# Joined: the output projection's low parts on VectorE between the norm's steps, with late modulation tiles, and substitution on blocks of 32 over 100 partitions

## The chip, the core and the metric

The kernel runs on one core of a Trainium2 chip. A core has a matrix engine (TensorE, PE in the profile, with its weight loads as PEld), three engines for elementwise work (VectorE or DVE, ScalarE or ACT, GpSimd or POOL), a queue engine that starts most transfers (SyncE or SP) and 16 DMA engines. The metric is the device time of one execution in microseconds (us); the median of several executions counts.

## What is computed

One layer of a streaming encoder for two sequences: 1024 tokens of a new stream ("prompt") and 64 tokens that follow 256 cached ones ("sample"). Width 1024; a conditioning vector per sequence gives six modulation vectors. The reference, cut to what the change touches:

```python
mod = jax.nn.silu(c) @ w_ada + b_ada
sh1, sc1, gt1, sh2, sc2, gt2 = jnp.split(mod, 6, axis=-1)
h = _rms_norm(x, norm1_g) * (1 + sc1[:, None]) + sh1[:, None]
proj = h @ w_in
...
def step(s, inp):
    r_t, w_t, k_t, v_t, kk_t, a_t = inp
    sa = jnp.einsum('bhvk,bhk->bhv', s, -kk_t)
    s = (s * w_t[:, :, None, :]
         + sa[..., None] * (kk_t * a_t)[:, :, None, :]
         + v_t[..., None] * k_t[:, :, None, :])
    return s, jnp.einsum('bhvk,bhk->bhv', s, r_t)
...
mix = jnp.concatenate([y_rwkv, y_fox], axis=-1) @ w_out
x = x + gt1[:, None] * mix
h2 = _rms_norm(x, norm2_g) * (1 + sc2[:, None]) + sh2[:, None]
ffn = (jax.nn.silu(h2 @ w_ffn_gate) * (h2 @ w_ffn_up)) @ w_ffn_down
x = x + gt2[:, None] * ffn
```

The recurrence `step` (8 heads of 64) is computed in chunks of 64 tokens. Within a chunk it needs the inverse of a 64 x 64 unit triangular matrix, one for each chunk and head.

## The kernel before

The tokens are worked in two halves, half 0 with 512 columns (8 chunks) and half 1 with 576 (8 chunks of the prompt and the sample as a ninth). All large products are in fp32r with each operand split into a high and a low part, so that one product is three matmuls: high by high, high by low, low by high (`mm3`, L294 to L296 for the projections). A weight tile is loaded to `wraw`, its high part `whi` is cast by ScalarE (L212), its low part `wlo` is the difference (L216), on VectorE or, with `pool_lo` set, on GpSimd.

The stages in the trace of before, in order: start and norm (0 to 42 us); the projections of both halves with the recurrence's blocks between them (42 to about 690); attention of both halves with the out projection of half 0 (700 to 940); the transition (940 to 1050: out projection of half 1, norm and operand sums `h2_make` of both halves, first FFN products); the FFN's gate and up products (1050 to 1490, `ffn`, in a Strassen-like form with the seven products of `fast_half`); the down projection (1490 to 1760). The projections' 1872 matmuls are called `pmm` in the profile, those of the out projection `po`, those of the FFN `pfa`, `pfb`, `pfc`, `pfe`, those of the down projection `pd`.

The modulation is 48 tiles of 128 columns of w_ada. A tile is 16 small matmuls (`pada`, L190) into four row groups, a copy `mrow`, a transpose on PE (L198) and a sum on VectorE. Tiles 0 to 15 are made at the start, tiles 16 to 47 stand in a list, `background`, from which the projections take one now and then. Tiles 40 to 47 hold gt2, which only the down projection reads.

The recurrence has four blocks j of two heads in each half: `rwkv_a` prepares a block, `rwkv_b` finishes it. In `rwkv_a` the products of keys, `pA` (L464), are masked into `At` (L466); for every chunk, head and half of a chunk the two 16 x 16 diagonal blocks go through DRAM (`dm`) into a layout with one block per partition (`mb`, 64 or 72 partitions), where VectorE inverts all of them at once by forward substitution: 15 steps of a product `tb` (L488) and an addition to `wb` (L490). The inverses and their transposes (L491) go through DRAM again (`dw`, `du`) and are gathered as `gt` and `inv` in `rwkv_b`. There three groups of 32 x 32 matmuls (in `small`, L523: pg1, pw1, pu1, in the profile `pg`, `pw` and `pu` with the operand `g`) join two 16-blocks to a 32-block, with a masked copy `g1` on VectorE (L530) and an addition (L535) between them; pgt and pu12 join two 32-blocks to a 64-block, and the recurrence over the chunks follows (`pR`, `pSA`, `pS`).

The order on each engine is fixed when the program is built: a framework emits the code in program order, every engine runs its own instructions in the order in which it got them, and waits by semaphores; tiles come from pools with a fixed number of buffers, and a load into a buffer waits for the last reader of the previous tile there. Transfers start in the order of SyncE's queue. Code that is to lie beside other code is written as a generator (`h2_make`, `fast_prep`), of which hooks take one step after each product.

In the transition of before, `h2_make(half 0)` is issued whole ahead of the out projection of half 1, whose low parts are on GpSimd (L216). `x1_sq` sums the squares of each finished column tile, `x1_rs` turns them to the norm's factor. `ffn` begins with half 0 of the first gate pair, during which `h2_make(half 1)` is worked off by a hook.

## Time and profile before

| quantity | value |
|---|---|
| median of 3 runs | 1759.04 us (1754.95 to 1759.44) |
| the profiled execution's own time | 1761.91 us |
| its span in the trace | 1760.2 us |
| mean granted clock of PE | 0.974 |
| moved by DMA | 207.10 MB |

The profile is of one execution. "Busy" is the time in which at least one instruction of an engine runs; waits do not count. Rows of instruction groups give line, engine, operation, output and inputs with their shape, count, busy time in us, mean ns of one, and the idle time of the engine just before them with what ended it. Rows of waits read: who waited, for whom, us, times, longest. Rows of the timeline start with start and length in us. The granted clock is that of PE, 1.00 being full speed.

### The profile page before, as it was taken

Reading aid. Unit: us, or ns where it says so; the run is one execution under the profiler, and the core shown is the slowest. Engines: PE = TensorE matmul, PEld = TensorE weight load, DVE = VectorE, ACT = ScalarE, POOL = GpSimd, SP = SyncE. Lnnn points to the kernel's source line nnn. Section 1 sums busy time; section 2 is a strip of 40 time slices with the busy share of each in tenths; the row PEclk is TensorE's granted clock in tenths of the full one; section 3 lists DMA queues with packets and bytes.
Section 4 is the critical chain, followed back from the end, with each engine's and each line's share of the span. In section 5 each row is a group of like instructions: output and inputs, shape, how many; then the busy total and the mean of one; then the engine's idle time right before and its main releaser. Section 6 shows DMA issues by size and latency. Waiting matters only on the chain.

```text
span 1760.2 us, 33567 instructions
## 1 busy us (share of the span) xinstructions
PE 1673.6 (95%) x12893; PEld 1454.0 (83%) x12893; DVE 1105.8 (63%) x2518; ACT 728.0 (41%) x1532; POOL 267.6 (15%) x468
## 2 busy tenths in 40 slices
PE   5999999999999998889999779999999999999999
PEld 3676666688888886666888779999999999999998
DVE  6676676757786753777876685556666654444434
ACT  4435454543555344566776363233333222112110
POOL 2102121121222122100212300000000000222221
PEclk9999999999999997889999899999999999999999
DMA  8435356642233336376663302222222224533313
GB/s 314 151 87 157 116 165 195 184 122 71 76 75 92 107 84 167 96 203 166 158 188 128 106 34 83 74 74 74 74 74 78 79 89 134 182 99 93 99 36 120
DMA packets 136143, 207.10 MB, mean 118 GB/s; under 512 B 64687, under 2 KB 72911, under 8 KB 135983
## 3 DMA queue, kind: packets, MB, share of 16 engines
q1 hardware_dynamic: 135982, 204.95, 39.1%
q8 instruction: 102, 1.67, 0.4%
q14 instruction: 59, 0.48, 0.1%
HBM read 157.65 MB, written 47.25 MB: 116 GB/s over the span
## 4 chain that ended last, share of the span: by engine, by line
PE 81%; DVE 7%; ACT 6%; issue 3%; DMA 3%; POOL 1%; SPq 0%; ACTq 0%; DVEq 0%; POOLq 0%
PE pd L1244 15%; PE pfc L1143 7%; PE pfe L1143 7%; PE pfa L1143 7%; PE pmm L294 5%; PE pmm L296 5%; PE pmm L295 5%; PE pfb L1143 4%; PE pav L952 2%; PE pbs L375 2%; PE ppt L930 2%; PE pA L464 2%; PE pS L613 1%; PE po L295 1%; PE po L294 1%
## 5 line engine op out<-in xcount | busy, mean ns | idle before, releaser
L216 POOL TENSOR_TENSOR wlo<-wraw,whi 128x512 fp32r<-128x512 f32 (+2 forms) x64 | 107.1, 1675 | 777.5 <-ACT whi L212 772.2
L294 PE MATMUL pmm<-hhi,whi 128*128 128x288 f32 (+1 forms) x624 | 220.3, 353 | 1.0 <-ACT pb L317 0.7
L295 PE MATMUL pmm<-hlo,whi 128*128 128x288 f32 (+1 forms) x624 | 216.8, 347 | 1.4 <-DVE hlo L272 1.4
L296 PE MATMUL pmm<-hhi,wlo 128*128 128x288 f32 (+1 forms) x624 | 215.6, 345 | 0.0
L212 ACT CAST whi<-wraw 128x1024 fp32r<-128x1024 f32 (+2 forms) x116 | 99.2, 855 | 234.8 <-PE pd L1244 168.1
L1244 PE MATMUL pd<-ah,whi 128*128 128x512 f32 (+1 forms) x528 | 173.3, 329 | 2.2 <-ACT ah L212 2.2
L1244 PE MATMUL pd<-al,whi 128*128 128x512 f32 (+1 forms) x528 | 174.1, 330 | 0.5 <-DVE al L216 0.5
L1244 PE MATMUL pd<-ah,wlo 128*128 128x512 f32 (+1 forms) x528 | 173.7, 329 | 0.0
L1248 DVE SCALAR_TENSOR_TENSOR x1t<-pd,mod,x1t 128x512 f32<-128x512 f32 x192 | 90.6, 497 | 132.1 <-PE pd L1244 131.0
L294 PEld LDWEIGHTS pmm<-hhi,whi 128*128 128x128 f32 x624 | 119.2, 191 | 14.3 <-ACT pb L317 2.5
L295 PEld LDWEIGHTS pmm<-hlo,whi 128*128 128x128 f32 x624 | 119.4, 191 | 11.1 <-DVE hlo L272 2.1
L296 PEld LDWEIGHTS pmm<-hhi,wlo 128*128 128x128 f32 x624 | 119.4, 191 | 10.2 <-issue 1.2
L1143 PE MATMUL pfc<-hh,hS 128*128 128x256 f32 (+1 forms) x352 | 102.3, 291 | 8.0 <-ACT hh L1045 5.6
L1244 PEld LDWEIGHTS pd<-ah,whi 128*128 128x128 f32 x528 | 99.8, 189 | 10.5 <-ACT ah L212 2.7
L1244 PEld LDWEIGHTS pd<-al,whi 128*128 128x128 f32 x528 | 99.8, 189 | 8.5 <-DVE al L216 0.7
L1244 PEld LDWEIGHTS pd<-ah,wlo 128*128 128x128 f32 x528 | 99.9, 189 | 7.5
L604 POOL TENSOR_SCALAR sd<-sv,pc 64x64 f32<-64x64 f32 x136 | 72.1, 530 | 202.7 <-DVE sv L617 190.3
L1143 PE MATMUL pfc<-hl,hS 128*128 128x256 f32 (+1 forms) x352 | 102.4, 291 | 0.0
L1143 PE MATMUL pfc<-hh,lS 128*128 128x256 f32 (+1 forms) x352 | 102.2, 290 | 0.0
L1143 PE MATMUL pfa<-hh,whi 128*128 128x256 f32 (+1 forms) x352 | 102.0, 290 | 0.0
L1143 PE MATMUL pfa<-hl,whi 128*128 128x256 f32 (+1 forms) x352 | 101.8, 289 | 0.0
L1143 PE MATMUL pfa<-hh,wlo 128*128 128x256 f32 (+1 forms) x352 | 101.4, 288 | 0.0
(360 smaller groups left out, 4471.6 us busy)
## 6 DMA issues: line engine op xcount, KB each, us to landing
wraw<-in_w_in_dram SPq DMA_DIRECT2D x52, 512.0 KB
wada<-in_w_ada_dram SPq DMA_DIRECT2D x48, 512.0 KB
as<-actscr SPq DMA_DIRECT2D x22, 544.0 KB
wraw<-in_w_gate_dram SPq DMA_DIRECT2D x22, 512.0 KB
wraw<-in_w_up_dram SPq DMA_DIRECT2D x22, 512.0 KB
wraw<-in_w_down_dram SPq DMA_DIRECT2D x40, 256.0 KB
wraw<-in_w_out_dram SPq DMA_DIRECT2D x16, 512.0 KB
actscr<-sg SPq DMA_DIRECT2D x22, 288.0 KB
```

Source lines behind the costliest of these rows:

```text
L212: nc.scalar.copy(hi, src)
L216: eng.tensor_tensor(lo, src, hi.bitcast(F32), op=ALU.subtract)
L294: nc.tensor.matmul(ps[0:M, 0:n], whi[:, k, 0:M], xhi[:, k, off:off + n], start=(k == 0), stop=False)
L295: nc.tensor.matmul(ps[0:M, 0:n], whi[:, k, 0:M], xlo[:, k, off:off + n], start=False, stop=False)
L296: nc.tensor.matmul(ps[0:M, 0:n], wlo[:, k, 0:M], xhi[:, k, off:off + n], start=False, stop=(k == kt - 1))
L375: nc.tensor.matmul(ps[:, 0:n], w, x[:, off:off + n], start=True, stop=True)
L464: nc.tensor.matmul(pa[h][:, i], kb[hp, c + i], rk[hp, c + i], start=True, stop=True)
L604: nc.gpsimd.tensor_scalar(sd[hsl[h]], sv[hsl[h], c, h], pc[hsl[h], c], None, op0=ALU.mult)
L930: nc.tensor.transpose(pt[0:rows, b - b0, t * P:t * P + qn], p[0:qn, b * P:b * P + rows], self.ident[0:qn, 0:qn])
L1143: nc.tensor.matmul(ps, l[:, k], r[:, s, k], start=(first and k == 0 and y == 0), stop=(k == 3 and y == 2), skip_group_check=True)
L1244: nc.tensor.matmul(ps[:, 0:n], w[:, i], x[:, t:t + n], start=(i == 0 and y == 0), stop=(i == len(fs) - 1 and y == 2))
L1248: nc.vector.scalar_tensor_tensor(dst, ps[:, so - off:so - off + l], self.mod[:, 40 + o, b:b + 1], dst, op0=ALU.mult, op1=ALU.add)
```

## The change

There are three parts.

Substitution. It runs on 32 x 32 diagonal blocks. Each block's inverse is held as two halves of 16 columns, one on partitions 0 to 31 (35 in half 1), one from partition 64 on, so that all instructions span 100 partitions; rows and columns are stored with even ones ahead of odd ones, and the two halves take the even and the odd columns, so that a step works on a rectangle that is the same for both. There are 31 steps of a product and an addition. The first operand `rk` and the mask `amask` are written in the permuted order. The tile `mb` is allocated once and cleared on GpSimd. pg1, pw1 and pu1 with their masked copy, addition and copies are gone, as are the transfers that cleared `dw` and `du`.

Transition. After attention, all low parts of weights are made on VectorE (this holds for the down projection's weights too). `h2_make(half 0)` is taken step by step between the column tiles of the out projection of half 1, the first two weight tiles of which are loaded ahead of it. w_gate's first pair is loaded and prepared one column tile earlier, w_up's first pair after the first half of the first FFN step.

Modulation and activations. Tiles 40 to 47 leave the background list. Tiles 40 to 43 are made behind `x1_rs` of half 1, tiles 44 to 47 behind half 0 of the first FFN step (`gap`). The first two activation tiles of the down projection are loaded at the last FFN step but one (`early`).

```diff
-                                        fill=0.0, base=0, pattern=[[1, 64]], channel_multiplier=-1)
+                                        fill=0.0, base=0, pattern=[[32, 2], [1, 2], [2, 16]], channel_multiplier=-1)
...
+        self.mb = r.tile([100, 32, 32], F32, name="mb", tag="mb")
+        nc.gpsimd.memset(self.mb, 0.0)
...
-        nc.vector.tensor_tensor(rk[:, 0:nch, 0:64], ch(kk), pp[:, 0:nch, 0:64], op=ALU.mult)
+        for x in (0, 32):
+            eo = lambda t: t[:, 0:nch, x:x + 32].rearrange("p c (t e) -> p c t e", e=2)
+            nc.vector.tensor_tensor(rk[:, 0:nch, x:x + 32].rearrange("p c (e t) -> p c t e", e=2), eo(ch(kk)), eo(pp), op=ALU.mult)
...
-        nb = 2 * ng
-        dm = self.dpool.tile([2, ng, 2, 16, 16], F32, tag="dm", name="dm")
+        nb = 2 * nch * 2
+        dm = self.dpool.tile([ng, 2, 32, 32], F32, tag="dm", name="dm")
         for h in range(2):
             for x in range(2):
-                for i in range(2):
-                    o = 32 * x + 16 * i
-                    nc.sync.dma_start(dm[i, h * nch:(h + 1) * nch, x].rearrange("g s t -> s g t"),
-                                      At[64 * h + o:64 * h + o + 16, 0:nch, 0, h, o:o + 16])
-        mb = self.rpool.tile([72, 16, 16], F32, tag="mb", name="mb")
-        nc.sync.dma_start(mb[0:2 * nb], dm.rearrange("i g x s t -> (i g x) s t"))
-        wb = self.rpool.tile([72, 16, 16], F32, tag="wb", name="wb")
-        tb = self.rpool.tile([72, 64], F32, tag="tb", name="tb")
-        nc.gpsimd.memset(wb[0:2 * nb], 0.0)
-        nc.gpsimd.affine_select(out=wb[0:2 * nb], in_=wb[0:2 * nb], compare_op=ALU.not_equal, fill=1.0, base=0,
-                                pattern=[[-1, 16], [1, 16]], channel_multiplier=0)
-        for s in range(15):
-            m = 15 - s
-            t_ = tb[0:2 * nb, 0:m * (s + 1)].rearrange("p (a b) -> p a b", b=s + 1)
-            nc.vector.tensor_tensor(t_, mb[0:2 * nb, s, s + 1:16].unsqueeze(2).to_broadcast([2 * nb, m, s + 1]),
-                                    wb[0:2 * nb, s:s + 1, 0:s + 1].to_broadcast([2 * nb, m, s + 1]), op=ALU.mult)
-            nc.vector.tensor_tensor(wb[0:2 * nb, s + 1:16, 0:s + 1], wb[0:2 * nb, s + 1:16, 0:s + 1], t_, op=ALU.add)
-        nc.vector.tensor_copy(mb[0:2 * nb], wb[0:2 * nb].rearrange("p s t -> p t s"))
+                o = 32 * x
+                nc.sync.dma_start(dm[h * nch:(h + 1) * nch, x].rearrange("g s t -> s g t"),
+                                  At[64 * h + o:64 * h + o + 32, 0:nch, 0, h, o:o + 32])
+        mb = self.mb
+        nc.gpsimd.memset(mb[32:64], 0.0)
+        if nb == 32:
+            nc.gpsimd.memset(mb[96:100], 0.0)
+        for p in (0, 64):
+            nc.sync.dma_start(mb[p:p + nb], dm.rearrange("g x s t -> (g x) s t"))
+        wb = self.rpool.tile([100, 32, 16], F32, tag="wb", name="wb")
+        tb = self.rpool.tile([100, 144], F32, tag="tb", name="tb")
+        nc.gpsimd.memset(wb, 0.0)
+        for p, n in ((0, 64), (64, 36)):
+            o = slice(p // 4, p // 4 + 16)
+            nc.gpsimd.affine_select(out=wb[p:p + n, o], in_=wb[p:p + n, o], compare_op=ALU.not_equal, fill=1.0,
+                                    base=0, pattern=[[1, 16], [-1, 16]], channel_multiplier=0)
+        m4 = mb.rearrange("p s (e t) -> p s e t", e=2)
+        w4 = wb.rearrange("p (e t) c -> p e t c", e=2)
+        for s in range(31):
+            o, e = (s + 1) // 2, s // 2 + 1
+            m, sh = 16 - o, [100, 2, 16 - o, e]
+            t_ = tb[:, 0:2 * m * e].rearrange("p (x a b) -> p x a b", x=2, b=e)
+            nc.vector.tensor_tensor(t_, m4[:, s, :, o:16].unsqueeze(3).to_broadcast(sh),
+                                    w4[:, s % 2, s // 2, 0:e].unsqueeze(1).unsqueeze(1).to_broadcast(sh), op=ALU.mult)
+            nc.vector.tensor_tensor(w4[:, :, o:16, 0:e], w4[:, :, o:16, 0:e], t_, op=ALU.add)
+        wt = mb.rearrange("p s t -> p (s t)")[:, 0:512].rearrange("p (s t) -> p s t", s=16)
+        nc.vector.tensor_copy(wt.rearrange("p s (t e) -> p s t e", e=2), wb.rearrange("p (e t) c -> p c t e", e=2))
 
         dw, du = [t[j % 2] for t in (self.dw, self.du)]
-        for i in range(2):
-            r, o = slice(i * nb, (i + 1) * nb), slice(16 * i, 16 * i + 16)
-            for d, t in ((dw, wb), (du, mb)):
-                nc.sync.dma_start(d[0:ng].rearrange("g x s t -> (g x) s t")[:, o, o], t[r])
+        for i, p in enumerate((0, 64)):
+            o = slice(16 * i, 16 * i + 16)
+            for e in range(2):
+                nc.sync.dma_start(dw[0:ng].rearrange("g x (s e) t -> (g x) e s t", e=2)[:, e, :, o],
+                                  wb[p:p + nb, 16 * e:16 * e + 16])
+            nc.sync.dma_start(du[0:ng].rearrange("g x s t -> (g x) s t")[:, o], wt[p:p + nb])
...
-        g1 = self.rpool.tile([P, 9, 32], F32, tag="g1", name="g1")
-        pg = small("pg1", (0, 1), lambda h, c, r, o: (At[r, c, 0, h, o], gt[r, c]))
-        for h in range(2):
-            hs = slice(64 * h, 64 * h + 64)
-            nc.vector.tensor_tensor(g1[hs, 0:nch], pg[h][hs, 0:nch],
-                                    self.qmask[hs].unsqueeze(1).to_broadcast([64, nch, 32]), op=ALU.mult)
-        pg = small("pw1", (0,), lambda h, c, r, o: (inv[r, c, r], g1[r, c]))
-        for h in range(2):
-            r = slice(64 * h, 64 * h + 32)
-            nc.vector.tensor_tensor(gt[r, 0:nch, 0:16], gt[r, 0:nch, 0:16], pg[h][r, 0:nch, 0:16], op=ALU.add)
-        pg = small("pu1", (0, 1), lambda h, c, r, o: (g1[r, c], inv[r, c, r]))
-        for h in range(2):
-            for x in range(2):
-                r = 64 * h + 32 * x
-                nc.scalar.copy(inv[r:r + 16, 0:nch, r + 16:r + 32], pg[h][r:r + 16, 0:nch, 16:32])
...
+            if i and i + 2 < len(src):
                 raw.append(self.fast_raw(src[i + 2]))
+            if i == len(src) - 2:
+                early()
             old, nw = gen, {}
-            gen = self.fast_prep(raw[i + 1], nw) if i + 1 < len(src) else iter(())
+            gen = self.fast_prep(raw[i + 1], nw) if 0 < i < len(src) - 1 else iter(())
...
+                    gap()
+                    raw.append(self.fast_raw(src[2]))
+                    gen = self.fast_prep(raw[1], nw)
...
-            self.background = [lambda t=t: self.ada_fin(self.ada_mm(t)) for t in range(16, 48)]
+            self.background = [lambda t=t: self.ada_fin(self.ada_mm(t)) for t in range(16, 40)]
...
+            self.pool_lo = False
             acc = None
             for o in range(KT):
                 acc = self.x1_sq(halves[0], o, acc)
-            for _ in self.h2_make(halves[0], self.x1_rs(halves[0], acc)):
-                pass
+            w1 = [self.load_w(A["w_out"][o], [P, KT, P]) for o in range(2)]
+            h2 = self.h2_make(halves[0], self.x1_rs(halves[0], acc))
             pair = lambda x: [A[x][i] for i in range(2)]
-            acc, raw, w = None, [], {}
+            acc, raw, w, ada = None, [], {}, []
             for o in range(KT):
-                self.outproj(halves[1], o, ("ab", "ce")[o % 2])
+                self.outproj(halves[1], o, ("ab", "ce")[o % 2], w1[o] if o < 2 else None)
                 acc = self.x1_sq(halves[1], o, acc)
+                next(h2, None)
+                if o in (0, 2):
+                    next(h2, None)
+                if o == 4:
+                    raw.append(self.fast_raw(pair("w_gate")))
                 if o == 5:
-                    raw.append(self.fast_raw(pair("w_gate")))
-                if o == 6:
                     for _ in self.fast_prep(raw[0], w):
                         pass
-            raw.append(self.fast_raw(pair("w_up")))
+            for _ in h2:
+                pass
+            ada = [(t, self.ada_load(t)) for t in range(40, 44)]
             rs = self.x1_rs(halves[1], acc)
+            def ada_run(part):
+                old = None
+                for t, r in part:
+                    new = self.ada_mm(t, r, "b")
+                    if old:
+                        self.ada_fin(old)
+                    old = new
+                self.ada_fin(old)
+            def gap():
+                ada_run(ada[4:])
+                raw.append(self.fast_raw(pair("w_up")))
+            ada_run(ada)
+            ada += [(t, self.ada_load(t)) for t in range(44, 48)]
...
+            early_s = top.enter_context(ExitStack())
+            def early():
+                h2s[2].close()
+                self.spool.pools["as"] = L(early_s, "sas0", 2)
+                for f in range(2):
+                    pre.append(self.act_load(f, None))
```

How the instructions move is shown at three places, as rows of each engine's program order (line, operation, output and inputs, shape, count of equal rows).

TensorE at the end of the projections' stage, in the last block of half 1. `pg`, `pw` and `pu` with the operand `g` are the three groups of the 32-column combine, `pgt` the product that first uses the block's inverse, `pkv` and `pkvs` transposes of attention's values, `plora` a projection of the last output gates. Before:

```order
L523 MATMUL pg_8390<-gt,At 32x32 x15
L523 MATMUL pw_8431<-g_8389,inv_693 32x32 x9
L523 MATMUL pu_8453<-inv_693,g_8389 32x32 x18
L523 MATMUL pw_8430<-g_8389,inv_693 32x32 x2
L817 MATMUL pkv<-ident,fv 128x128 x4
L523 MATMUL pw_8430<-g_8389,inv_693 32x32 x7
L523 MATMUL pgt<-gt,At 32x32 x9
L523 MATMUL pu_8452<-inv_693,g_8389 32x32 x16
L823 MATMUL pkvs<-ident,fv 64x128
L523 MATMUL pu_8452<-inv_693,g_8389 32x32 x2
L549 MATMUL pu_8517<-inv_693,gt 32x32 x9
L523 MATMUL pgt<-gt,At 32x32 x9
```

After:

```order
L362 MATMUL plora<-z,wg 128x288
L810 MATMUL pkv<-ident,fv 128x128 x4
L362 MATMUL plora<-z,wg 128x288
L816 MATMUL pkvs<-ident,fv 64x128
L532 MATMUL pgt<-gt,At 32x32 x9
L542 MATMUL pu_7855<-inv_690,gt 32x32 x9
L532 MATMUL pgt<-gt,At 32x32 x9
L560 MATMUL pkbt<-ident,kb 128x128 x9
L542 MATMUL pu_7856<-inv_690,gt 32x32 x9
```

The three groups are gone; `pgt` now directly follows the gathered inverse.

VectorE in the transition, during the norm of half 0. `x_0` is half 0's tile, of which L1040 makes the norm and L1044 (after: L1037) the differences and low parts; L992 (after: L985) adds a finished out projection of half 1 to `x_1`. Before:

```order
L992 SCALAR_TENSOR_TENSOR x_1_11730<-po,mod,x_1_11730 128x224
L992 SCALAR_TENSOR_TENSOR x_1_11730<-po,mod,x_1_11730 128x64
L1040 SCALAR_TENSOR_TENSOR x_0_9704<-x_0_9704,g_162,nrs 128x512 x8
L992 SCALAR_TENSOR_TENSOR x_1_11730<-po,mod,x_1_11730 128x224
L992 SCALAR_TENSOR_TENSOR x_1_11730<-po,mod,x_1_11730 128x64
L1044 TENSOR_TENSOR hl_11726<-x_0_9704,hh_11725 128x1024
L992 SCALAR_TENSOR_TENSOR x_1_11730<-po,mod,x_1_11730 128x288
L1044 TENSOR_TENSOR x_0_9704<-x_0_9704 128x4x256
```

After:

```order
L1037 TENSOR_TENSOR x_0_9042<-x_0_9042 128x4x256
L216 TENSOR_TENSOR wlo<-wraw,whi 128x1024
L995 TENSOR_TENSOR nsq<-nsq 128x576
L1037 TENSOR_TENSOR hl_11070<-x_0_9042,hh_11069 128x1024 x2
L1037 TENSOR_TENSOR x_0_9042<-x_0_9042 128x4x256
L985 SCALAR_TENSOR_TENSOR x_1_11074<-po,mod,x_1_11074 128x288
L216 TENSOR_TENSOR wlo<-wraw,whi 128x1024
```

The low parts of w_out (`wlo`), which before stand on GpSimd, now stand on VectorE between the norm's steps.

TensorE in the first FFN step, half 0, at the passage from the product `pfe` to the product `pfb`. Before:

```order
L1143 MATMUL pfe<-hl_11726,hS_12268 128x256
L1143 MATMUL pfe<-hh_11725,lS_12269 128x256
L1143 MATMUL pfb<-hh_11725,hS_12264 128x256
L1143 MATMUL pfb<-hl_11726,hS_12264 128x256
L1143 MATMUL pfb<-hh_11725,lS_12265 128x256
```

After (L1136 is L1143 of before):

```order
L1136 MATMUL pfe<-hl_11070,hS_11547 128x256
L1136 MATMUL pfe<-hh_11069,lS_11548 128x256
L190 MATMUL pada<-wada,ct 32x128 x16
L198 MATMUL pada<-ident,mrow 128x128 x2
L190 MATMUL pada<-wada,ct 32x128 x16
L198 MATMUL pada<-ident,mrow 128x128 x2
L1136 MATMUL pfb<-hh_11069,hS_11543 128x256
L1136 MATMUL pfb<-hl_11070,hS_11543 128x256
```

Modulation tiles now stand between two of the step's products.

More of the change, by code (lines that the diff above doesn't have):

```diff
@@ L87, in consts @@
         nc.vector.reciprocal(sg, sg)
-        self.ct = self.cmid.tile([P, KT, 32], F32, name="ct")
+        self.ct = c.tile([P, KT, 32], F32, name="ct")
         nc.gpsimd.memset(self.ct, 0.0)
@@ L344, in rwkv_persist @@
         self.gt = r.tile([P, 9, 32], F32, name="gt", tag="gt")
-        self.qmask = self.fper.tile([P, 32], F32, name="qmask")
-        nc.vector.tensor_reduce(self.qmask[:, 0:1], self.ident.rearrange("p (q i s) -> p i q s", i=2, s=16)[:, 1],
-                                axis=AX.XY, op=ALU.add)
-        nc.vector.tensor_copy(self.qmask[:, 1:16], self.qmask[:, 0:1].to_broadcast([P, 15]))
-        nc.gpsimd.memset(self.qmask[:, 16:32], 0.0)
-        zero = self.inv[0].rearrange("p c t -> p (c t)")[0:72, 0:512]
-        for t in self.dw + self.du:
-            nc.sync.dma_start(t.rearrange("g x s t -> (g x s t)").rearrange("(p t) -> p t", p=72), zero)
+        self.mb = r.tile([100, 32, 32], F32, name="mb", tag="mb")
+        nc.gpsimd.memset(self.mb, 0.0)
         self.pp = r.tile([P, 9, 65], F32, name="pp", tag="pp")
@@ L975, in load_mix, with outproj @@
             self.split(mh[:, m, 0:n], ml[:, m, 0:n], t[:, 0:n], pool_lo=False)
-    def outproj(self, hf, o, tags=("mm",)):
-        wh, wl = self.load_w(self.A["w_out"][o], [P, KT, P])
+    def outproj(self, hf, o, tags=("mm",), w=None):
+        wh, wl = w or self.load_w(self.A["w_out"][o], [P, KT, P])
         for x, (off, n) in enumerate(hf.chunks):
@@ L1157, in fast_half, with ffn @@
                 h(x)
-    def ffn(self, halves, raw, w, h2gen, mid):
+    def ffn(self, halves, raw, w, h2gen, gap, early, mid):
         nc, A = self.nc, self.A
@@ L1197, in out, with prep @@
                                           sg[hf.i][:, 2 * q - 2:2 * q].rearrange("p q t -> p (q t)"))
-                hooks = [lambda x: next(gen, None) if self.STEPS[hf.i][x] else None]
+                def prep(x):
+                    for _ in range((0, 0, 0, 3, 2, 2, 1)[x] if i == 0 else self.STEPS[hf.i][x]):
+                        next(gen, None)
+                hooks = [prep]
                 if hf.i == 0:
@@ L1493, in x1_load @@
                     nc.sync.dma_start(x1a[o][:, hf.t0:hf.t0 + hf.n], self.x1scr[hf.i][:, o])
+            early_s = top.enter_context(ExitStack())
[4 more added lines that the diff above has]
+                    pre.append(self.act_load(f, None))
             def mid(x):
                 if x == 0:
-                    h2s[2].close()
                     h2s[0].close()
-                    self.spool.pools["as"] = R(ds, "sas", 2)
                     apools.append(MultiPool({t: R(ds, t + "0", 4) for t in ("ah", "al")}))
                     self.x1pools = [MultiPool({"x1": R(ds, "x1a", 4)})]
-                if x in (0, 1):
-                    pre.append(self.act_load(x, apools[0]))
-                if x in (3, 4):
-                    pre[x - 3] = self.act_split(pre[x - 3])
-                    pre.append(self.act_load(x - 1, apools[0]))
-                if x == 5:
+                    self.spool.pools["as"] = R(ds, "sas", 2)
+                    for f in range(2, 4):
+                        pre.append(self.act_load(f, None))
                     x1_load(0, self.x1pools[0])
-                if x == 6:
-                    pre[2] = self.act_split(pre[2])
-            self.ffn(halves, raw, w, self.h2_make(halves[1], rs), mid)
-            pre[3] = self.act_split(pre[3])
+                if 0 < x < 5:
+                    pre[x - 1] = self.act_split((pre[x - 1][0], apools[0]))
+            self.ffn(halves, raw, w, self.h2_make(halves[1], rs), gap, early, mid)
+            early_s.close()
             h2s[1].close()
```

5 lines of the change are left out of this document (2 added, 3 removed).

## The prediction

> **What bounds the kernel now.** First the page's busy shares and its slices, to see which engine has no room and where it does; then the chain of work that ended last.
>
> ```profile
> PE 1673.6 (95%) x12893; PEld 1454.0 (83%) x12893; DVE 1105.8 (63%) x2518; ACT 728.0 (41%) x1532; POOL 267.6 (15%) x468
> PE   5999999999999998889999779999999999999999
> DVE  6676676757786753777876685556666654444434
> PEclk9999999999999997889999899999999999999999
> PE 81%; DVE 7%; ACT 6%; issue 3%; DMA 3%; POOL 1%; SPq 0%; ACTq 0%; DVEq 0%; POOLq 0%
> ```
>
> TensorE (PE) is busy for 95% of the span, with dips only in slice 1, slices 16 to 18 and slices 23 and 24; 81% of the chain is PE. So whatever PE need no longer do counts in full, work that can be moved into the dips counts too, and work added to another engine counts only where PE has to wait for it. The change does all three: it takes matmuls out of the projections' stage, moves others into the dip near 1000 us, and loads VectorE (DVE). The next view is busy time by stretches over the projections' stage, 88 to 690 us (columns: stretch, length, busy time and instructions of PE, weight loads, DVE, ACT, POOL; granted clock, DMA share, GB/s).
>
> ```profile
> 88.00:264.00 176.00, 171.50 (x1411) 122.41 (x1411) 124.63 (x345) 81.08 (x169) 32.07 (x70) 0.98 0.46 131
> 264.00:396.00 132.00, 125.02 (x1162) 97.16 (x1160) 84.71 (x234) 66.92 (x158) 26.72 (x60) 0.95 0.58 167
> 396.00:572.00 176.00, 173.05 (x1670) 148.34 (x1668) 132.67 (x371) 84.52 (x199) 39.58 (x85) 1.00 0.31 79
> 572.00:690.00 118.00, 114.86 (x1149) 98.02 (x1148) 66.38 (x180) 54.02 (x131) 26.82 (x47) 0.98 0.38 106
> sum 602.00, PE 584.42 PEld 465.93 DVE 408.38 ACT 286.54 POOL 125.19; mean PE 146.11 PEld 116.48 DVE 102.09 ACT 71.64 POOL 31.30
> ```
>
> PE stands idle there for 17.6 of 602 us, while DVE is 68% busy: PE bounds this stage, and DVE has 194 us of room in it.
>
> **Term 1, the 32-column combine leaves PE.** Three groups of small matmuls go, all 1360 of them (pgt and what follows it stay). Their busy time counts overlapping pipeline time; what one keeps the next from is read in the timeline, where 30 run in a row and the next matmul starts.
>
> ```profile
> L523 PE MATMUL pg<-gt,At 32*32 32x32 f32 x544 | 13.5, 193 | 0.0
> L523 PE MATMUL pu<-inv,g 32*32 32x32 f32 x544 | 12.9, 193 | 0.0
> L523 PE MATMUL pw<-g,inv 32*32 32x32 f32 x272 | 11.6, 195 | 0.5 <-DVE g L530 0.5
> 132.10 0.69 PE L523 MATMUL pg<-gt,At 32*32 32x32 f32 x30
> 132.72 0.53 PE L190 MATMUL pada<-wada,ct 128*32 128x128 f32 x12
> ```
>
> From 132.10 to 132.72 is 0.62 us for 30, 20.7 ns each; 1360 of them are 28.1 us. The upper end is the busy time, 13.5 + 12.9 + 11.6 = 38.0. I take **−28**, the start-to-start figure, as that is what the next instruction sees. The Trainium skill (TensorE: Matmul & The Clock Gate, section "Wait — 56ns, not 53.3ns?") says that starts never follow each other closer than about 25 ns; by it the group would be 34 us, an estimate from that page, and the sum 6 us lower. The trace's 20.7 ns lies under that floor, and the row decides.
>
> **Term 2, modulation tiles into the dip.** Eight tiles (of 48, 16 matmuls and one transpose each) leave the projections' stage for the transition, where the order puts them between the last out projection and the first FFN products.
>
> ```profile
> L190 PE MATMUL pada<-wada,ct 128*32 128x128 f32 x768 | 37.0, 290 | 12.5 <-DMA wada<-in_w_ada_dram 10.8 <-DVE mod L201 1.0 <-DVE x L270 0.4
> L198 PE MATMUL pada<-ident,mrow 128*128 128x128 f32 x48 | 14.3, 298 | 4.0 <-ACT mrow L193 3.9
> 1010.00:1020.00 10.00, 7.64 (x58) 7.02 (x56) 5.57 (x11) 8.40 (x11) 0.00 (x0) 1.00 0.13 50
> 1020.00:1030.00 10.00, 6.40 (x48) 5.94 (x48) 9.65 (x20) 9.41 (x21) 0.00 (x0) 1.00 0.00 0
> 1030.00:1040.00 10.00, 6.31 (x26) 5.99 (x27) 10.00 (x8) 6.80 (x8) 0.00 (x0) 0.66 0.01 2
> ```
>
> A tile is 37.0/48 = 0.77 us of PE; eight are 6.2, with their transposes (14.3/48 = 0.30 each) 8.6. Their cover is PE's idle time from 1010 to 1040, 2.36 + 3.60 + 3.69 = 9.65 us; DMA is nearly idle there, so the weights can land. Without that cover they cost the same 6.2 as before, and the gain is 0. I take **−6**, bounds 0 to −8.6.
>
> **Term 3, low parts from POOL to DVE.** PE's longest wait of the transition is for a low part of w_out.
>
> ```profile
> PE po L296 <- POOL wlo L216: 10.2, 2, 8.8
> 969.98 12.13 POOL L216 TENSOR_TENSOR wlo<-wraw,whi 128x1024 fp32r<-128x1024 f32 x2 [9.30 <-ACT whi L212]
> 952.69 2.38 POOL L216 TENSOR_TENSOR wlo<-wraw,whi 128x1024 fp32r<-128x1024 f32 x1 [9.17 <-ACT whi L212]
> L216 DVE TENSOR_TENSOR wlo<-wraw,whi 128x1024 fp32r<-128x1024 f32 x52 | 63.4, 1219 | 23.9 <-ACT whi L212 23.0 <-DMA dm<-At 0.6
> 970.00:980.00 10.00, 1.18 (x5) 0.94 (x6) 9.98 (x12) 4.15 (x5) 10.00 (x2) 0.73 0.00 0
> 980.00:990.00 10.00, 10.00 (x61) 10.00 (x60) 1.24 (x4) 1.64 (x2) 2.85 (x2) 0.76 0.54 164
> ```
>
> Two waits, 10.2 us. POOL needs 2.38 us for one low part, but two took 12.13 while DVE was 9.98 of 10 busy with the norm of half 0; DVE does one in 1.22. The clock falls to 0.76 behind the gap: (1 − 0.76) × 10 = 2.4 us more. In all 12.6. But the DVE that is now to make the parts is the one that was full: eight parts are 9.8 us added where it had no room, so if the norm keeps its place in front of them the gain is gone. The order puts single low parts between the norm's steps (two or three instructions of the size in row L216, 2.4 to 3.7 us), so PE waits for about one step. I take 12.6 less that step and a little of the clock, **−8**, bounds −12.6 to 0. POOL's 48 other low parts (those of w_down) also move to DVE; they stand two column tiles ahead of use, where the slices show DVE at 3 to 4 tenths: nothing.
>
> **Term 4, the joint of FFN and down projection.** Two activations are now loaded one step earlier.
>
> ```profile
> PE pd L1244 <- ACT ah L212: 2.2, 1, 2.2
> 1490.00:1500.00 10.00, 7.25 (x32) 5.89 (x31) 4.70 (x7) 3.24 (x3) 0.00 (x0) 0.84 0.91 290
> ```
>
> PE idles 2.75 us and loses (1 − 0.84) × 10 = 1.6 to the clock, with the DMA engines 0.91 full: an early load removes most. **−3**, bounds 0 to −4.4.
>
> **Term 5, the longer chain on DVE.** The substitution on blocks of 32 has 31 steps, 62 instructions, for the 30 of before. Durations by size:
>
> ```profile
> L488 DVE TENSOR_TENSOR tb<-mb,wb 64x15 f32<-64x15 f32 x8 | 1.3, 160 | 0.1
> L488 DVE TENSOR_TENSOR tb<-mb,wb 64x63 f32<-64x63 f32 x8 | 1.7, 213 | 0.2
> L490 DVE TENSOR_TENSOR wb<-wb,tb 64x15 f32<-64x15 f32 x8 | 1.4, 169 | 0.2
> L490 DVE TENSOR_TENSOR wb<-wb,tb 64x63 f32<-64x63 f32 x8 | 1.7, 212 | 0.1
> L488 DVE TENSOR_TENSOR tb<-mb,wb 64x15 f32<-64x15 f32 (+15 forms) x120 | 24.7, 206 | 3.3 <-DMA mb<-dm 1.2
> L490 DVE TENSOR_TENSOR wb<-wb,tb 64x15 f32<-64x15 f32 (+15 forms) x120 | 23.9, 199 | 2.7
> L530 DVE TENSOR_TENSOR g<-pg,qmask 64x256 f32<-64x256 f32 (+1 forms) x16 | 7.0, 436 | 5.2 <-PE pg L523 4.9
> L535 DVE TENSOR_TENSOR gt<-gt,pw 32x128 f32<-32x128 f32 (+1 forms) x16 | 4.6, 287 | 4.5 <-PE pw L523 4.3
> ```
>
> The products cost 143 ns + 1.10 per element, the additions 156 + 0.90. The new steps have 2992 elements a side in all (the sum over s of 2 × (16 − o) × e of the code): 31 × 143 + 2992 × 1.10 = 7.7 us and 31 × 156 + 2992 × 0.90 = 7.5, together 15.2 for the 48.6/8 = 6.1 of before. So +9.1 us a block and, with about 30 ns between instructions, 10 us later at the end of the chain. No row has 100 partitions; 64 and 72 cost alike, so I add nothing. L530 and L535 go (11.6/8 = 1.45), a wider copy and the split product rk add some 0.4: net +8 a block, 65 in all. DVE is then 473 of 602 − 34 = 568 us, 83%, in the second half (132.67 + 66.38 + 32 = 231) of 277 (294 less half of the 34), 83%. What it costs is the wait at the end of the chain:
>
> ```profile
> 122.27 0.17 DVE L490 TENSOR_TENSOR wb<-wb,tb 64x15 f32<-64x15 f32 x1
> 130.10 0.24 PE L523 MATMUL pg<-gt,At 32*32 32x32 f32 x2
> 288.04 0.17 DVE L490 TENSOR_TENSOR wb<-wb,tb 64x15 f32<-64x15 f32 x1
> 330.82 0.35 PE L523 MATMUL pg<-gt,At 32*32 32x32 f32 x10
> ```
>
> From the chain's end to its first use lie 7.7 us in the first block and 42 in the fourth. In the changed order the first use of block 0 stands behind 311 projection matmuls for 264 before, and in the second half behind 1230 for 1113; at 602/1872 = 0.32 us of stage for each of the 1872, that is 15 and 38 us later, more than the 10 added. So the chain is mostly covered; what stays is that everything else on DVE queues behind 62 short instructions instead of 30 (the 52 low parts of row L216 among it). Lower end −10: the granted clocks of 0.98, 0.95 and 0.98 in three of the four stretches stand for 171.50 × 0.02 + 125.02 × 0.05 + 114.86 × 0.02 = 12 us of PE time, some of which may come back with the short waits between the removed groups. Upper end +42: four blocks of eight exposed. I take **+7**, nearer the covered end, as the rows give slack in most blocks.
>
> **Sum.** −28 − 6 − 8 − 3 + 7 = −38. The profiled execution took 1761.9 us: 1723.9. The median of the three runs shown is 2.9 lower: **1721**.
>
> **Rivals.**
> *The transition gives nothing.* DVE is at 9.65 to 10.00 of 10 in 970 to 980 and 1020 to 1040. If terms 2 to 4 all come back as waits for DVE, −28 + 7 = −21 remain: 1738, up to 1752 if DVE queues in the first stage as well. Against it: once interleaved, the norm of half 0 is not needed before the first FFN products, past 1000 us, and DVE has 8.76 us free in 980 to 990 alone. Chance 0.16.
> *Slower: PE waits out the longer chain.* Place: the first product on the inverse (pgt) in each block; price 10.2 us a block. With all eight exposed +82 − 45 = +37, 1796; it gives a slower kernel from five blocks on (51 − 45 = 6). For it: 7.7 us of slack in block 0, and DVE at 83%. Against: 42 us in block 3, and the later first use. The Trainium skill (VectorE: DVE Perf Modes, "Rules for kernel authors") tells authors of chained DVE instructions to minimise their number; this change doubles it, and by that rule this rival would hold. The trace agrees as to price, 143 of 160 ns being independent of size. Chance 0.10.
> *More gain than taken.* Term 1 at 38 and term 3 in full: under 1700. Chance 0.10.
> *No change to be measured.* Chance 0.06. That the change doesn't do what it says is excluded by the order: the small matmuls are gone and the modulation rows stand in the transition.
>
> **The numbers.** Forecast 1700 to 1740, 0.58; the others as given. 0.3% (5.3 us) is about what a measurement of this kernel can tell from no change. Faster by more: 0.58 + 0.10 + 0.16 = 0.84; the same 0.06; slower 0.10. The range 1690 to 1752 leaves out the cases of no change and slower and the far end of the best.
>
> **What would show it.** Right: no pg, pu, pw of 32x32 on g; stage 88 to 690 about 27 to 34 us shorter with PE still over 95%; DVE near 83% in it; no wait of `po` over 4 us; the dip at 1010 to 1040 filled with `pada`. Wrong: waits of pmm for `hlo` or `wlo`, or of pgt for the transfer behind `wb`, of tens of us; DVE over 15 us a block more; a gap of PE after 1000 us larger than 10 us.

## The result, and the profile after

| kernel | median us | runs | to the kernel before [95% interval] |
|---|---|---|---|
| before | 1759.11 | 8 | 1 |
| after | 1771.84 (1761.93 to 1776.50) | 8 | 1.0066 [1.0039, 1.0094] |

The change made the kernel slower by 0.66%, some 12 us, where 38 us less had been forecast. The page of the changed kernel, the same rows as before (its execution took 1771.66 us):

```profile
span 1770.0 us, 30815 instructions
PE 1659.1 (94%) x11533; PEld 1444.3 (82%) x11533; DVE 1183.5 (67%) x2804; ACT 721.7 (41%) x1500; POOL 211.3 (12%) x432
PE   6998997999899987788999889999999999999999
DVE  5886796777967856486786876555555666555545
PEclk8998996999899988698999989999999999999999
PE 79%; DVE 10%; ACT 5%; issue 3%; DMA 2%; SPq 0%; POOL 0%; DVEq 0%; ACTq 0%; POOLq 0%
```

PE has 1360 instructions less, yet only 14.5 us less busy time, and the row of the granted clock has 8s and a 6 in its first 15 slices, where there were only 9s. The mean clock over the span fell from 0.974 to 0.956. The records of these runs know only full and half speed, so over the span that is 2 × 0.026 × 1760 = 92 us at half speed before and 2 × 0.044 × 1770 = 156 after: 64 us more, worth up to 32 us of PE. The projections' stage by the same stretches:

```profile
88.00:264.00 176.00, 165.61 (x1050) 118.38 (x1049) 138.58 (x421) 75.63 (x156) 44.78 (x82) 0.95 0.42 126
264.00:396.00 132.00, 117.77 (x760) 90.31 (x761) 90.62 (x245) 64.49 (x141) 29.11 (x55) 0.88 0.54 161
396.00:572.00 176.00, 167.29 (x1235) 144.52 (x1234) 135.79 (x378) 72.28 (x162) 42.23 (x83) 0.94 0.27 74
572.00:690.00 118.00, 105.41 (x710) 88.51 (x709) 85.97 (x277) 54.99 (x135) 30.26 (x49) 0.92 0.33 96
```

The clock column was 0.98, 0.95, 1.00, 0.98, and PE idles 45.9 us of 602 where it idled 17.6. The last projection matmul starts at 699.0 us for 679.1 before: the stage that was to be 27 us shorter is 20 longer. What follows gives some of that back: the last out projection ends 11.2 us later than before, the last matmul of all 9.5. The waits of PE in the stage, longest total first, of before (its first row) and of the changed kernel:

```profile
PE pu L549 <- ACT gt L545: 2.2, 3, 1.5
```

```profile
PE pbs L369 <- DVE z L448: 6.9, 3, 2.8
PE pmm L294 <- ACT whi L212: 6.7, 2, 6.1
PE pS L606 <- ACT sv L605: 4.5, 7, 1.2
PE pmm L296 <- DVE wlo L216: 3.5, 1, 3.5
```

`z` is an operand that VectorE makes for each block, `sv` a vector of the recurrence. Of 43.0 us in all such rows of the stage, 15.7 end with VectorE and 27.3 with ScalarE, where before had 4.3 and 8.6. So the larger part is put down to ScalarE, whose own load did not grow; how much of it goes back to VectorE in its turn is not shown. The 6.1 us for `whi` end with a cast that had itself waited for the transfer of its weight tile.

One more wait, longer than any of these, stands just behind the last projection matmul, in the last block of half 1. The kernel before has none like it, nor have the runs with a shorter chain, e3 and e9 below:

```profile
PE pgt L532 <- DMA gt<-dw: 9.3, 1, 9.3
711.53 0.54 SPq L522 DMA_DIRECT2D gt<-dw  x1
713.58 1.14 PE L532 MATMUL pgt<-gt,At 32*32 32x32 f32 x18 [9.31 <-DMA gt<-dw]
```

This is PE waiting for the block's inverse. Its chain had ended at 687.2 us, but SyncE started the gathering transfers only from 711.5 us on, behind other transfers in its queue.

One of the waits in the list, in the timeline and in windows around it:

```profile
264.61 1.13 PE L369 MATMUL pbs<-z,bones 128*128 128x512 f32 x2 [2.47 <-DVE z L448]
255.00:262.00 7.00, 6.90 (x26) 4.24 (x24) 6.94 (x17) 3.84 (x5) 2.50 (x4) 1.00 0.63 171
262.00:265.60 3.60, 1.13 (x3) 0.30 (x2) 3.54 (x7) 0.00 (x0) 1.48 (x2) 1.00 0.34 96
265.60:286.00 20.40, 18.82 (x103) 13.63 (x103) 10.42 (x18) 6.95 (x13) 1.73 (x3) 0.50 0.55 173
```

PE waits 2.47 us for `z` while VectorE is full (6.94 of 7.00, 3.54 of 3.60 us), and the clock is 0.50 for the next 20.4 us, in which PE is busy for 18.8. The wait costs 2.5 us, the clock behind it up to 9 (an estimate, half of the 18.8). VectorE is full because the chain of block 2 ended just ahead; its first and last instruction, before and after:

```profile
210.45 0.16 DVE L488 TENSOR_TENSOR tb<-mb,wb 64x15 f32<-64x15 f32 x1
220.53 0.17 DVE L490 TENSOR_TENSOR wb<-wb,tb 64x15 f32<-64x15 f32 x1
```

```profile
222.52 0.18 DVE L494 TENSOR_TENSOR tb<-mb,wb 100x32 f32<-100x32 f32 x1
256.01 0.18 DVE L496 TENSOR_TENSOR wb<-wb,tb 100x32 f32<-100x32 f32 x1
L496 DVE TENSOR_TENSOR wb<-wb,tb 100x120 f32<-100x120 f32 (+14 forms) x248 | 65.7, 265 | 4.0
L494 DVE TENSOR_TENSOR tb<-mb,wb 100x120 f32<-100x120 f32 (+14 forms) x248 | 63.0, 254 | 4.1
```

From 10.3 us the chain has grown to 33.7, though its own busy time is (65.7 + 63.0)/8 = 16.1 us: other work stands between its steps. Over the eight blocks it lasts 29 to 42 us (34.9 on average), for 9 to 18 (12.6) before.

### The profile page after: what moved, and what is told of

The parts are those of the page before. It is cut to its first block, busy times and chain, and to the rows that moved or that the text cites. A ratio compares the mean times of both kernels' runs of the same rounds, so it can differ in the third digit from the quotient of the medians.

```text
span 1770.0 us, 30815 instructions
## 1 busy us (share of the span) xinstructions
PE 1659.1 (94%) x11533; PEld 1444.3 (82%) x11533; DVE 1183.5 (67%) x2804; ACT 721.7 (41%) x1500; POOL 211.3 (12%) x432
## 4 chain that ended last, share of the span: by engine, by line
PE 79%; DVE 10%; ACT 5%; issue 3%; DMA 2%; SPq 0%; POOL 0%; DVEq 0%; ACTq 0%; POOLq 0%
PE pd L1247 15%; PE pfc L1136 7%; PE pfe L1136 7%; PE pfa L1136 7%; PE pmm L294 4%; PE pmm L296 4%; PE pmm L295 4%; PE pfb L1136 4%; PE pav L945 2%; PE ppt L923 2%; PE pbs L369 2%; DMA wada<-in_w_ada_dram 2%; PE pA L461 2%; PE po L295 2%; PE po L294 2%
## 5 line engine op out<-in xcount | busy, mean ns | idle before, releaser
L216 DVE TENSOR_TENSOR wlo<-wraw,whi 128x1024 fp32r<-128x1024 f32 (+2 forms) x108 | 103.7, 960 | 12.8 <-ACT whi L212 12.5
L597 POOL TENSOR_SCALAR sd<-sv,pc 64x64 f32<-64x64 f32 x136 | 81.2, 597 | 204.9 <-DVE sv L610 178.7
L1136 PE MATMUL pfc<-hh,hS 128*128 128x256 f32 (+1 forms) x352 | 101.6, 289 | 4.0 <-ACT hh L1038 4.0
L1136 PE MATMUL pfc<-hl,hS 128*128 128x256 f32 (+1 forms) x352 | 102.0, 290 | 0.0
L1136 PE MATMUL pfa<-hl,whi 128*128 128x256 f32 (+1 forms) x352 | 101.8, 289 | 0.0
L1136 PE MATMUL pfc<-hh,lS 128*128 128x256 f32 (+1 forms) x352 | 101.7, 289 | 0.0
L1136 PE MATMUL pfa<-hh,whi 128*128 128x256 f32 (+1 forms) x352 | 101.7, 289 | 0.0
L1136 PE MATMUL pfa<-hh,wlo 128*128 128x256 f32 (+1 forms) x352 | 101.4, 288 | 0.0
```

What stands on the lines that cost most here:

```text
L216: eng.tensor_tensor(lo, src, hi.bitcast(F32), op=ALU.subtract)
L597: nc.gpsimd.tensor_scalar(sd[hsl[h]], sv[hsl[h], c, h], pc[hsl[h], c], None, op0=ALU.mult)
L1136: nc.tensor.matmul(ps, l[:, k], r[:, s, k], start=(first and k == 0 and y == 0), stop=(k == 3 and y == 2), skip_group_check=True)
```

## The experiments

Theory 1: the longer chain on VectorE makes PE wait, and the clock falls behind the waits. Theory 2: the removed matmuls and modulation tiles had filled PE's waits, and without them it idles. Kernels of a group ran with the kernel before on one chip; ratios go to that, and 1% is 17.6 us.

| run | median us | ratio [95% interval] | median clock |
|---|---|---|---|
| e1 substitution alone | 1772.67 | 1.0072 [1.0045, 1.0100] | 0.959 |
| e2 all but the substitution | 1762.44 | 1.0009 [0.9986, 1.0032] | 0.970 |
| e3 after, 15 of 31 steps | 1732.27 | 0.9846 [0.9814, 0.9878] | 0.974 |
| e4 before, longer chain | 1770.76 | 1.0058 [1.0034, 1.0081] | 0.968 |
| e5 after, eight tiles back | 1764.64 | 1.0030 [1.0013, 1.0048] | 0.960 |
| e6 transition and joint alone | 1747.89 | 0.9941 [0.9919, 0.9964] | 0.978 |
| e7 half of w_in's low parts on GpSimd | 1808.57 | 1.0278 [1.0250, 1.0305] | 0.952 |
| e8 small matmuls put back | 1800.61 | 1.0231 [1.0203, 1.0258] | 0.952 |
| e9 after, 23 of 31 steps | 1756.92 | 1.0001 [0.9984, 1.0017] | 0.962 |
| e10 chain later | 1774.14 | 1.0094 [1.0072, 1.0115] | 0.960 |
| e11 chain latest | 1816.19 | 1.0319 [1.0294, 1.0344] | 0.945 |
| e12 eight tiles left out | 1757.38 | 0.9990 [0.9970, 1.0009] | 0.972 |
| e13 e5, copies to ScalarE | 1747.99 | 0.9934 [0.9916, 0.9952] | 0.971 |
| e14 e6, copies to ScalarE | 1763.45 | 1.0021 [1.0001, 1.0041] | 0.970 |
| e15 eight tiles made twice | 1754.14 | 0.9966 [0.9951, 0.9982] | 0.975 |

**Which part.** e1 and e2 split the diff: e1 is the kernel before with the diff's parts in `rwkv_persist`, `rwkv_a` and `rwkv_b`, e2 has all the others.

> The kernel before with the substitution part alone (32-blocks, no 32-column combine), 32 modulation tiles left in the projections' stage, transition as before. Theory 1 (the longer chain on VectorE makes PE wait for other VectorE results and PE's granted clock falls with the waits): the whole loss is in this part, 1775 to 1790 us, half-clock time in 88 to 730 us of 90 us or more for 55 before. Theory 2 (the removed matmuls and modulation tiles had filled PE's waits; without fillers it idles and the clock falls): with the 8 tiles back in place most of the loss is gone, 1750 to 1765.

> The kernel before with everything but the substitution part: low parts on VectorE, norm interleaved, 24 modulation tiles in the projections' stage and 8 late, early activation loads. Theory 1: the gains of the transition and the joint stay and nothing else is lost, 1738 to 1748 us. Theory 2: the stage loses its fillers here too, so that the gain of the transition (8 us) and of the joint (4 us) is eaten by half-clock time, 1752 to 1762.

e1 alone is as slow as the whole change, as theory 1 said, though its 1772.67 us lie just under the 1775 to 1790 given. e2 is no faster than before, as theory 2 said, just past its 1752 to 1762. Both theories failed once, and the rest of the change holds a loss of its own.

**The chain's length.** e3 and e9 shorten it to 15 and 23 steps, so that the inverses are incomplete; e4 lengthens that of the kernel before. The edit of e3, and that of e4 at the chain:

```diff
-        for s in range(31):
+        for s in range(15):
```

```diff
+        wv, tv, zz = wb[0:2 * nb, 0:4], tb[0:2 * nb, 0:64].rearrange("p (s t) -> p s t", t=16), self.zz[0:2 * nb]
+        for s in range(21):
+            nc.vector.tensor_tensor(tv, wv, zz, op=ALU.mult)
+            nc.vector.tensor_tensor(wv, wv, tv, op=ALU.add)
```

> The changed kernel with 15 of the 31 steps of the substitution (steps 15 to 30 left out, so the inverses are incomplete): PE's work is that of the change, VectorE's chain has 30 instructions again. Theory 1: the loss goes and the gain of the removed matmuls shows, 1715 to 1732 us. Theory 2: the fillers are still missing, 1755 to 1775.

> The kernel before with 21 more pairs of a product with zeros and an addition at the end of each block's substitution (42 instructions of 64 elements, about 0.215 us each, 9 us a block), nothing else changed. Theory 1: the longer chain costs by itself 20 to 40 us, 1780 to 1800. Theory 2: PE's work and fillers are those of before, so the chain hides, 1757 to 1768.

> The changed kernel with 23 of the 31 steps (steps 23 to 30 left out, so the inverses are incomplete): 46 of 62 instructions, between the changed kernel and the run with the short chain. If each us of VectorE's chain has the same price (39 us for 8.2 us a block): 1748 to 1757 us. If most of the chain is covered and only its last part exposed: 1732 to 1742. If there is a step early on: 1762 or more.

With the short chain (7.6 us busy a block) the changed kernel takes 1.54% less than before; 23 steps (12.2 us) bring 27 us of that back and the last eight (to 16.1) some 11 more by the ratios (0.9846, 1.0001, 1.0066), 39 us for 8.5 us of VectorE a block: 3 to 6 us for each us added to a block, from the first on. The waits of e3 in the stage:

```profile
PE pS L606 <- ACT sv L605: 3.3, 5, 1.1
PE pR L590 <- ACT sv L571: 1.6, 3, 0.9
PE pmm L295 <- DVE hlo L272: 1.4, 3, 0.7
```

Those for `z`, `whi` and `wlo` have gone to 1.0 us and less, and the clock is back at 0.974. In e4 the chains are about as long as in the changed kernel (28 to 39 us, with 15.4 us of instructions a block) but PE's work is untouched, and it loses only 10 us, half of the least that theory 1 wanted and more than theory 2 allowed. So the chain's price depends on what stands around it; on what, was not shown.

**The small matmuls.** e8 puts them back, read by nobody.

```diff
+        small("pg1", (0, 1), lambda h, c, r, o: (At[r, c, 0, h, o], gt[r, c]))
+        small("pw1", (0,), lambda h, c, r, o: (inv[r, c, r], gt[r, c]))
+        small("pu1", (0, 1), lambda h, c, r, o: (gt[r, c], inv[r, c, r]))
```

> The changed kernel with the 1360 small matmuls put back at their place in each block, their results read by nobody (so without the copies and additions between them): only PE's work is added. Theory 1: they cost what they cost before, 28 us, 1793 to 1803. Theory 2: they keep the clock up and cost little or nothing, 1762 to 1780.

They cost 1.65%, 29 us more than the changed kernel. As fillers they are worth nothing: they keep no clock up, and one bunch of them was followed by half clock (windows of e8):

```profile
512.00:516.00 4.00, 4.00 (x115) 3.28 (x114) 0.00 (x0) 0.00 (x0) 0.00 (x0) 0.99 0.55 136
516.00:520.00 4.00, 3.97 (x74) 3.01 (x73) 0.75 (x2) 2.03 (x4) 1.89 (x3) 0.50 0.63 168
```

The rows show PE busy throughout, mostly with 32x32 matmuls, and the clock halves all the same. So a part of the 29 us is clock (median 0.952 for 0.956), and 28 us as the price of the group, with its own place in the kernel before, is neither more nor less than consistent with it.

**The eight tiles.** e5 puts tiles 40 to 47 back into the background list of the changed kernel, e6 into that of e2; e12 leaves them out of e6 (gt2 set to ones), e15 makes them in both places.

```diff
-            self.background = [lambda t=t: self.ada_fin(self.ada_mm(t)) for t in range(16, 40)]
+            self.background = [lambda t=t: self.ada_fin(self.ada_mm(t)) for t in range(16, 48)]
```

> The changed kernel with modulation tiles 40 to 47 back in the background list (32 tiles in the projections' stage, none in the transition). Theory 1 (the loss is the longer chain on VectorE, whose waits also lower PE's granted clock): the tiles cost about what they save elsewhere, 1768 to 1778 us. Theory 2 (PE lacks filler matmuls while it waits): eight fillers back win part of the clock, 1757 to 1766.

> The kernel before with low parts on VectorE between the norm's steps and the early activation loads alone: neither the substitution part nor the late modulation tiles. If the nought of the run with everything but the substitution came from the eight tiles taken out of the projections' stage (theory 2): the transition's gain of 8 us and the joint's of 4 show, 1744 to 1753. If the transition's gain is itself given back (theory 3): 1757 to 1764.

> The run with the transition alone (before, with low parts on VectorE between the norm's steps and early activation loads), with modulation tiles 40 to 47 left out altogether (gt2 set to ones, so the outputs are not the layer's). Theory 2 (the background tiles are fillers whose loss lowers the clock in the projections' stage): no gain or a loss, 1747 to 1760 for the 1748 with them. If the eight tiles cost PE time in the stage and late ones cost it in the transition: 1738 to 1745.

> The run with everything but the substitution, with tiles 40 to 47 made twice: in the background of the projections' stage as before, and again late in the transition (the same values). If the tiles' going from the stage is what cost (theory 2, as the run without them says): 1747 to 1754 us, in spite of the added work. If the late tiles cost in the transition: 1762 or more, as in the run with them late only.

With the tiles back the transition's gain shows in full: e6 is 0.59% (10 us) faster than before. Against it, leaving the tiles out of the stage costs 0.49% though PE does less (e12), and making them late costs 0.25% (e15, at the edge of what was expected, with an interval that overlaps that of e6); e2 with both is 0.68% above e6. In the changed kernel the move costs 0.36% (after against e5, whose intervals overlap a little). Theory 2 fits these matmuls, 16 in a row that wait only for a load: the median clock goes from 0.978 to 0.972 and 0.970 without them. That they act as fillers and not by the altered order around them was not separated.

**Place of the chain, and load beside it.** e10 and e11 split the substitution off `rwkv_a` and give it out later; e7 and e13 take work off VectorE in the stage, by way of GpSimd and of ScalarE; e14 is e13's move without the long chain.

```diff
-            nc.vector.tensor_scalar(z[:, o:o + l], pb[:, 1 + b + o:1 + b + o + l], om, None, op0=ALU.mult)
+            nc.scalar.activation(z[:, o:o + l], pb[:, 1 + b + o:1 + b + o + l], AF.Identity, scale=om)
...
-        nc.vector.tensor_scalar(a[:, 0:n], a[:, 0:n], col(V_KA), self.oka[:, j:j + 1], op0=ALU.mult, op1=ALU.add)
+        nc.scalar.activation(a[:, 0:n], a[:, 0:n], AF.Identity, scale=col(V_KA), bias=self.oka[:, j:j + 1])
...
-                for h, cp in enumerate((nc.scalar.copy, nc.vector.tensor_copy)):
+                for h, cp in enumerate((nc.scalar.copy, nc.scalar.copy)):
...
-            nc.vector.tensor_copy(d[:, :, 0], s[:, :, h])
+            nc.scalar.copy(d[:, :, 0], s[:, :, h])
```

> The changed kernel with every second low part of w_in on GpSimd instead of VectorE during the projections' stage (26 of 52, some 32 us less of VectorE there; PE's work and order of program as in the change). Theory 1: VectorE's load is what makes PE wait, 1740 to 1758 us. Theory 2: VectorE's load does not matter, 1768 to 1778.

> The changed kernel with the eight tiles back in the projections' stage, and the substitution of each block given out a few tasks later in the program (behind the next block's projections or the next transposes), so that VectorE takes other work first; the same instructions, only their order differs. Theory 1a (the loss is other VectorE work of the stage that is held up behind the 62 instructions): 1740 to 1758, and the waits of PE for z on VectorE shrink. Theory 1b (VectorE's load as such): 1760 to 1770, as with the tiles back. Theory 1c (the chain's end is what PE waits for): 1772 or more.

> The same with each block's substitution given out just ahead of the block's second part, the latest place there is. Theory 1a: 1740 to 1758. Theory 1b: 1760 to 1770. Theory 1c: 1775 or more, with waits of PE for the gathered inverse.

> The changed kernel with the eight tiles back in the projections' stage, and four groups of copies and scalings of that stage moved from VectorE to ScalarE (z's scaling L331, a's L442, half of the copies of y L616, the casts L802: 32.6 us of VectorE in the run with the tiles back). If VectorE's load around the chains is what makes the chain last 30 to 42 us instead of its 17.5 (theory 1b): 1735 to 1755 us, each chain some us shorter. If the 62 dependent steps and their transfers themselves are what counts, whatever stands beside them: 1760 to 1770. If ScalarE becomes the next engine to wait for: 1770 or more.

> The same four groups moved to ScalarE in the run with the transition alone (16-blocks, short chain). Theory 1b: VectorE has room there, so nothing is won, 1744 to 1752 us; slower than 1753 if ScalarE's copies come late for PE.

e7 was a miss: 2.1%, 37 us slower than the changed kernel. It is confounded and tells nothing of VectorE's load: a low part takes GpSimd 2.4 us and more, and beside it the chains' own instructions take VectorE 146.9 us for 128.7. PE itself waits only 1.6 us for GpSimd's low parts. Later places are worse, so holding up other work (theory 1a) is not all of it. They are as slow as theory 1c said, but PE's waits for the gathered inverse come to only 10.0 us in e10 and 13.6 in e11. In e11 every chain ends 8 to 11 us ahead of its first use, and the transfers between them take about as long. The fourth block's last step and first use there:

```profile
381.80 0.19 DVE L502 TENSOR_TENSOR wb<-wb,tb 100x32 f32<-100x32 f32 x1
391.81 0.69 PE L538 MATMUL pgt<-gt,At 32*32 32x32 f32 x16 [0.40 <-DMA gt<-dw]
```

e13 answers whether VectorE's load costs: 33 us of it moved to ScalarE win 0.96% (17 us) where the chain is long (e5 to e13), and lose 0.80% (14 us) where it is short (e6 to e14). The stage of e5, then of e13, 88 to 690 us:

```profile
88.00:690.00 602.00, 563.05 (x3943) 448.71 (x3941) 457.03 (x1343) 273.85 (x609) 142.21 (x270) 0.95 0.41 121
```

```profile
88.00:690.00 602.00, 565.01 (x3974) 449.31 (x3972) 440.41 (x1272) 317.97 (x713) 149.90 (x277) 0.96 0.44 125
```

VectorE has 17 us less, ScalarE 44 more, and PE does more of its work in the same time. The chains hardly became shorter, against what was expected: 28 to 39 us, 32.4 on average for 34.3 in e5. What went down are PE's waits for other results, those for `whi` from 6.7 to 1.0 us and those for `z` from 3.4 to 1.9; the wait of the last block for its inverse stays (8.4 us for 9.2). e13 and e6 both beat both kernels, by 0.66% and 0.59% against before; with intervals that overlap, which is the better was not settled.

## Why the prediction was wrong, by its own steps

- **Bounds.** That PE bounds the stage held for the kernel before. "DVE has 194 us of room in it" was read from a mean over 602 us. Where the chains run there was much less, in the rows of before and after for the same two stretches:

```profile
222.00:262.00 40.00, 38.59 (x245) 25.68 (x244) 31.23 (x72) 22.90 (x44) 9.80 (x19) 1.00 0.59 163
446.00:486.00 40.00, 39.36 (x473) 33.24 (x472) 29.13 (x59) 21.79 (x51) 10.40 (x20) 1.00 0.24 54
```

```profile
222.00:262.00 40.00, 38.59 (x219) 27.04 (x217) 37.38 (x125) 22.43 (x45) 12.18 (x22) 1.00 0.42 121
446.00:486.00 40.00, 33.12 (x202) 27.99 (x201) 38.35 (x110) 19.57 (x36) 4.35 (x9) 0.89 0.13 38
```

 VectorE was at 78% and 73% there and is now at 93% and 96%; the forecast mean of 83% (75% was measured) hid it.
- **Term 1 (−28)** is borne out as far as the runs go. The kernel with the short chain is 27 us under before; it also has the transition and the joint (−10 by e6) and the moved tiles (+6 to +12), which leaves −23 to −29 as an estimate. e8 pays 29 us for the group's return, part of it clock.
- **Term 2 (−6)** had the wrong sign: moving the tiles cost 6 us (with the long chain) to 12 us (without). Its step that failed is "without that cover they cost the same 6.2 as before": in the projections' stage they cost nothing, their leaving did (e12: 9 us). Whether the idle time that was to take them took all is not settled (e15: 4 us, at the edge of the noise).
- **Terms 3 and 4 (−8 and −3)** were right together: e6 has both and gains 10 us; no run has one alone. In the changed kernel's transition the wait for a low part is 2.3 us for 10.2, and at the joint, now at 1503.8 us, PE is busy without a gap:

```profile
PE po L296 <- DVE wlo L216: 2.3, 1, 2.3
1500.00:1510.00 10.00, 10.00 (x65) 9.25 (x65) 7.25 (x12) 3.20 (x5) 0.00 (x0) 1.00 0.95 311
```

- **Term 5 (+7)** is the step that failed most: of the 51 us between forecast and result it makes 32, term 2 12 to 18. Its instruction price held (16.1 us a block for the 15.2 of the working), its cost was 39 us between e3 and the changed kernel, near the upper bound of 42 that was given and not chosen. Three things in its working were wrong. The chain was taken as "10 us later", its own instructions with 30 ns between them; it became 16 to 28 us longer from block to block, since VectorE's other work stands between the steps. Slack was priced at the first use of the inverse alone. It was there in most blocks (19 us lie between the end of the chain shown above, 256.2, and its first use at 275.5), but the transfers in between need some 10 of it, and in the last block PE waited 9.3 us. And that "everything else on DVE queues behind 62 short instructions" was named and got no price of its own: the wait for `z` shown above is of this kind.
- **The clock** was given as a possible gain, "some of which may come back". It fell from 0.974 to 0.956. Multiplying each median by a median clock (0.973 for before, from its runs beside e3) gives a rough time at full speed: 1712 before, 1694 after, 1686 for e3. By that reckoning, an estimate and an upper bound since PE isn't always busy, the change took 18 us of work away and 31 us came back through the clock.
- **The slower rival** named the right engine and condition ("PE waits out the longer chain"); it had a chance of 0.10. Its place, the first product on the inverse, is right for one block of eight, where PE waits 9.3 us for the 10.2 given; the rest of the loss lies elsewhere. Even with the chain in its latest place (e11, 56 us slower than before) only 13.6 us of waits lie there. The rule of the Trainium skill put beside it (VectorE: DVE Perf Modes, "Rules for kernel authors", to minimise the number of chained instructions) pointed the right way: e3 and e9 show that number's price here.
- The sum of the parts agrees with the whole: substitution +0.72% (e1), transition and joint −0.59% (e6), tiles +0.36% (after to e5), together +0.49%, or with +0.68% for the tiles (e2 to e6) +0.81%, for +0.66% measured.

What stays open: how the 39 us divide between waits and clock, since no run could hold the clock; how much of ScalarE's share in the waits goes back to VectorE; and why the same load on VectorE costs 10 us in e4 and 39 us here. PE has 28 us more of its own work there, which fits, but e8 has that work too and did not get the 29 us back: the order of the program differs in all three.

## What to carry to other kernels

Work moved from the bound engine to one with room on average is paid for where the room is missing: read the receiving engine's share in the very stretches in which the new work will run, count a chain by how long it lasts among its neighbours there, not by its own instructions, and price what queues beside it. The length alone is not the price: chains of that length cost 10 us in e4, and e13 won 17 us with hardly shorter ones. Where a short wait of the matrix engine is followed by a long stretch at half clock, as at 265 us here, it is charged several times over, so small independent matmuls in a stage full of short waits may be worth more than the time they take (the tiles of e12 seem to have been, the group of e8 was not). A joint change is best run in its parts first: here one part gained 10 us and the two others lost them and 12 more.

## What the runs showed of the hardware

- A wait of PE of 2.47 us was followed by 20.4 us at a clock of 0.50 (rows at 262 to 286 us). The Trainium skill (TensorE: Matmul & The Clock Gate, "Part 1: The HAM clock gate (the "warmup" mystery)") describes a gate that watches PE's activity in windows of about 3.4 us and passes full or half clock, half after an idle window; the trace agrees with the two values, but here a wait shorter than such a window was enough.
- A bunch of mostly 32x32 matmuls was followed by the same drop with no idle time in the profile's rows: PE busy 4.00 of 4.00 us, then 0.50 (e8).
- Executions of one program differ by more than 10 us, the longer ones at a lower clock: the changed kernel's ran from 1761.93 us at a clock of 0.966 to 1776.50 us at 0.951.
